# One decoder block: head-norm scaling placed one head later, gate weight sums in other slots, sum groups of 5, 5, 3 and 5

## The chip, the cores and the metric

One core of a Trainium2 chip runs the whole block. The metric is device time in microseconds (us). A run of the kernel before is given as the median of 3 runs with the lowest and the highest. Of one execution there is a profile with a trace, whose times count from the start of its span.

## The reference, cut to what matters

Batch 1, 512 tokens and 16 meta tokens ahead of them (528 positions), model width 1024, all in float32.

```
u    = rmsnorm(h, norm1_w)
proj = u @ w_in                       # q, f, i, g of HGRN2; z, xBC, dt of Mamba-2
out_a = hgrn2(q, f, i, g)             # 8 heads of 128
        # per head: o = linear recurrence(q, f, i)
        # o = o * rsqrt(mean(o*o) + eps) * norm_w * silu(g)
out_b = mamba2(z, xBC, dt)            # 16 heads of 64
h = h + concat(out_a, out_b) @ w_out
h = h + (silu(conv3(n @ w_up)[gate]) * conv3(n @ w_up)[val]) @ w_down,  n = rmsnorm(h, norm2_w)
y = rmsnorm(h, final_norm_w)[:, 16:]
```

The part at hand is the per-head norm of HGRN2 (`rsqrt(mean(o*o) + eps) * norm_w`), the gate `silu(g)`, and the weights of the gates and of the up-projection.

## The kernel before, in words

**Tiling.** Activations lie transposed, a tile is 128 channels by 528 positions. Weights come from HBM in tiles of 128 by 1024 (512 KB). A float32 product is made of three TensorE (PE) products of rounded halves: each weight tile `raw_` is split by ScalarE (ACT, line 212: `whi_`) and VectorE (DVE, line 213: `wlo_`), and each activation into `_hi` and `_lo` likewise. `ahead` (278) emits the load and split of two weight tiles ahead of their use. All weight loads go through the SyncE queue (SP).

**Order of the phases.** The first projections and Mamba-2 (to about 235 us of the span), then eight HGRN2 heads (`hgrn_head`, line 754) until about 425 us, the four gate pairs (loop at line 979), the output projection (`add_row`, 896), the up-projection (`conv3` for pairs 0 to 3, `scheme` for 4 to 21), the down-projection.

**A head.** `hgrn_head` projects f, q and i, makes decays on DVE, transposes v and k on PE (`pv`, `pk`, `pm`), copies them back on ACT (`vt`, `kt`, `mt`), forms scores on PE (`pa`, `pb`, and two columns in `pm`), masks them on DVE (line 853 writes the mask into `mt`), and multiplies (`po`, and line 866 into `pm`). ACT copies the result to `o`.

**The norm of four heads.** After heads 3 and 7 `hgrn_norm` (line 875) squares the four `o` on ACT (`osq`), sums them over channels on PE (`ph`, `phm`), takes the reciprocal root (`rh`), and then for each head stores one row to HBM (`rs_d`, line 889), loads it back spread over 128 partitions (`rb`, line 891), and multiplies `o` by it on DVE (line 892). The DMAs are SP's.

**Sums of weights.** The gates (4 pairs) and the up-projection's pairs 4 to 21 use a product scheme with seven instead of eight block products; it needs sums of weight blocks. `weight_sums` (232) makes them by accumulating DMAs from HBM to HBM (`sumsg_i`, `sums4` to `sums21`), issued by GpSimd (POOL) in groups. A group starts when a value named by its second argument is there: DVE copies a column of it into `ticks`, POOL copies that (line 237) and issues the group's DMAs, of which each stage needs the stage before. Groups of up-projection pairs before: 4 to 7 behind `ys[7]`, 8 to 11 behind `hs[3]`, 12 to 15 behind the output of head 4, 16 to 21 behind the output of head 7.

**Loading the sums.** `scheme_weights` (259) loads three tiles `w0`, `w2`, `w1` per pair, and with `w1` a fourth sum `s4` of 128 by 512 (256 KB), which is split into `s4h` (ACT, line 221) and `s4l` (DVE, line 222). All three `s4` tiles take slots of tag `ab`, of which there are 5; the heads' `vt`, `kt` and `S` use them too.

**The gates.** Per pair, PE forms blocks x, z, y, v in the order of lines 994 to 1012; ACT copies (`seed`, line 963) carry x into y and y into z; `sg` and `sgv` are the gates, multiplied into `o` on DVE (1018, 1019), and the products split into `oa`. `s4h`, `s4l` are used last, in z.

**What sets the order.** The program is written in a logical order; a scheduler with a cost model orders each engine's instructions by its own estimate of when they can start, so an edit may move nothing, or move things that it doesn't touch. Each engine then runs its list strictly in that order: an instruction that waits holds up all behind it on that engine.

Of the kernel before, what the change touches and what calls it, by code (L numbers as in the profile page):

```python
# [8 lines left out]
F32R = mybir.dt.float32r  # L9
# [45 lines left out]
DN = 1, 2, 3  # L55
D0, DK = 8, 6
NG = NH // 2
GROUPS = [("g", i) for i in range(NG)], WS[0:4], WS[4:8], WS[8:12], WS[12:], [("dn", 1)], [("dn", 2)], [("dn", 3)]
HT = 258
USUMS = {4: (0, 1), 5: (2,), 6: (3,)}  # L60
ROWS = {1: range(0, 4), 2: range(4, 8)}
NUNSC = 5

# [4 lines left out]
def tile_block(ctx: ExitStack, tc: tile.TileContext, xT, w_in, w_dt, w_out, w_up, w_down,  # L68
# [12 lines left out]
    def slot(name, n=NT, dtype=F32, parts=P, tag="m"):  # L81
        return gp.tile([parts, n], dtype, tag=tag, name=name, bufs=TAGS[tag])
# [29 lines left out]
    def col(c):  # L112
        return pt[:, c:c + 1]
# [146 lines left out]
    def scheme_weights(key):  # L260

        kind, j = key
        raw = raw_tile(key)
        hi, lo = split_tiles(key)
        if kind == "w0":
            nc.sync.dma_start(raw[:], pair_of(j)[0])
        elif kind == "w2":
            nc.sync.dma_start(raw[:], sumd[j][:, 0:2 * HK])
        else:
            n = "_".join(map(str, j)) if isinstance(j, tuple) else j  # L270
            s4 = slot(f"s4_{n}", 512, tag="ab")
            nc.sync.dma_start(s4[:], sumd[j][:, 3 * HK:])
            nc.sync.dma_start(raw[:, 0:HK], sumd[j][:, 2 * HK:3 * HK])
            nc.sync.dma_start(raw[:, HK:], pair_of(j)[1][:, HK:])
        split_weights(raw, hi, lo, slice(0, 2 * HK), V)
        if kind != "w1":
            return hi, lo
        h4, l4 = slot(f"s4h_{n}", 512, F32R, tag="ab"), slot(f"s4l_{n}", 512, F32R, tag="ab")
        last_s4[:] = [split_half(s4[:], h4[:], l4[:])]
        return hi, lo, h4, l4  # L280

# [471 lines left out]
    os_ = []  # L753
# [118 lines left out]

    rs_d = dp.tile([NH, NT], F32, name="rs_d")

    def hgrn_norm(h0):

        p0, p1 = bank(f"ph{h0}"), bank(f"phm{h0}")
        for e in range(4):
            o = os_[h0 + e]
            sq = slot(f"osq{h0 + e}", tag="L")  # L880
            A.activation(sq[:, T0:], o[:, T0:], AF.Square)
            PE.matmul(p0[32 * e:32 * e + 32, :], ones[:, 0:32], sq[:, META:], start=True, stop=True)
            PE.matmul(p1[32 * e:32 * e + 32, 0:2], ones[:, 0:32], sq[:, T0:META], start=True, stop=True)
        r = slot(f"rh{h0}", tag="L")
        log_exp(r, ((slice(T0, META), p1[:, 0:2]), (slice(META, NT), p0[:])), T0, 1.0 / P)
        for e in range(4):
            h = h0 + e
            o = os_[h]
            nc.sync.dma_start(rs_d[h:h + 1, T0:], r[32 * e:32 * e + 1, T0:])
            rb = slot(f"rb{h}", tag="L")  # L890
            nc.sync.dma_start(rb[:, T0:], rs_d[h:h + 1, T0:].partition_broadcast(P))
            V.scalar_tensor_tensor(o[:, T0:], o[:, T0:], col(C_HN + h), rb[:, T0:], ALU.mult, ALU.mult)

    tails = (slice(T0, T0 + HT), slice(NT - HT, NT))
# [42 lines left out]
    for h in range(NH):  # L937
        hgrn_head(h)
        for j in ROWS.get(h, ()):
            add_row(j, 1, obh, obl)  # L940
            if j == 3:
                weight_sums(GROUPS[2], hs[j])
        if h % 4 == 3:
            hgrn_norm(h - 3)
        for k in USUMS.get(h, ()):
            normed_sums(k)
        if h == 4:
            weight_sums(GROUPS[3], os_[h])
    weight_sums(GROUPS[4], os_[7])

    def mul(ps, hi, lo, xs, start=False):

# [23 lines left out]
    for i in range(NG):  # L976
# [38 lines left out]
        for h, g in ((2 * i, sg), (2 * i + 1, sv)):  # L1015
# [6 lines left out]
            dump(f"oa{h}", o[:])  # L1022
            oah.append(hi)
            oal.append(lo)

    u2h, u2l = [], []
    acc = None
# [383 lines left out]
```

## Time and profile before

| | |
|---|---|
| median of 3 runs | 885.41 us (882.82 to 886.45) |
| the profiled execution | 885.82 us, span 884.0 us |
| PE busy | 844.8 us (96%) |
| DVE, ACT, POOL busy | 642.1, 500.1, 140.0 us |
| mean granted TensorE clock | 0.986 |
| bytes moved by DMA | 168.73 MB, of them 62.53 MB by POOL's queue (q0) and 101.52 MB by SP's and the like (q1) |

A row of the timeline reads: start, duration, engine, line, operation, written tile <- read tiles, shapes, count, and in brackets the idle time of that engine before it and what ended that. A row of the waits reads: what waited, `<-` what for, us in total, times, longest. Buffer numbers are left out there, so `o` is any head's output and `s_g` any gate's `s4`. Rows that give "SPq" or "POOL ... DMA" show the issue of a DMA, not its transfer.

### The profile page before, as it was taken

To read this page: it belongs to the slowest core of one execution; us is meant where nothing else is said; L and a number is where in the kernel's file an instruction comes from. 1 tells how busy PE (TensorE), PEld (TensorE's weight loads), DVE (VectorE), ACT (ScalarE), POOL (GpSimd) and SP (SyncE) were. 2 spreads that over 40 slices of the span, in tenths; PEclk is the share of its full clock that TensorE was granted. 3 is DMA by queue.
4 is the path that set the end of the run, shared out by engine and by line. 5 is a ranking of instruction groups with operands and counts; after the bars stand their busy time and mean duration, and the time that the engine had idled before them with its cause. 6 is when DMAs were issued, how large, how long until landed. Compare 5 with 4: busy or idle time off the path is not lost. (4 is left out here: it accounts for less than half of the span.)

```text
span 884.0 us, 17041 instructions
## 1 busy us (share of the span) xinstructions
PE 844.8 (96%) x6864; PEld 813.1 (92%) x6864; DVE 642.1 (73%) x1106; ACT 500.1 (57%) x805; POOL 140.0 (16%) x182
## 2 busy tenths in 40 slices
PE   6999999999999994999789999999999999999996
PEld 6998898999999994999689999989999999889985
DVE  6985968788463663987366569978988888985535
ACT  8628975966232362454365555556766666764433
POOL 1300221223223212323112222200000000200000
PEclk9999999999999997899999999999999999999999
DMA  7584798886989988888669898955555555845543
GB/s 250 166 200 148 207 282 238 175 161 199 219 192 199 267 150 180 266 156 166 153 175 373 216 207 158 202 160 191 180 171 188 186 187 165 214 119 149 157 137 125
DMA packets 65839, 168.73 MB, mean 191 GB/s; under 512 B 6856, under 2 KB 11336, under 8 KB 65760
## 3 DMA queue, kind: packets, MB, share of 16 engines
q0 software_dynamic: 24800, 62.53, 36.2%
q1 hardware_dynamic: 38432, 101.52, 35.3%
q10 hardware_dynamic: 2528, 3.60, 1.2%
q8 instruction: 54, 0.88, 0.4%
q14 instruction: 25, 0.20, 0.1%
HBM read 165.47 MB, written 64.67 MB: 260 GB/s over the span
## 5 line engine op out<-in xcount | busy, mean ns | idle before, releaser
L339 PE MATMUL pj<-u_hi,whi_in 128*128 128x272 f32 (+1 forms) x624 | 132.7, 291 | 0.0
L339 PE MATMUL pj<-u_lo,whi_in 128*128 128x272 f32 (+1 forms) x624 | 131.1, 289 | 0.0
L339 PE MATMUL pj<-u_hi,wlo_in 128*128 128x272 f32 (+1 forms) x624 | 129.3, 287 | 0.0
L339 PEld LDWEIGHTS pj<-u_hi,whi_in 128*128 128x128 f32 x624 | 97.4, 190 | 2.9 <-issue 2.7
L339 PEld LDWEIGHTS pj<-u_lo,whi_in 128*128 128x128 f32 x624 | 97.4, 190 | 2.1 <-issue 1.8
L339 PEld LDWEIGHTS pj<-u_hi,wlo_in 128*128 128x128 f32 x624 | 97.2, 190 | 1.4 <-issue 1.3
L212 ACT ACTIVATE whi_in<-raw_in 128x1024 fp32r<-128x1024 f32 (+1 forms) x50 | 47.5, 951 | 73.7 <-PE pj L339 46.5
L213 DVE TENSOR_TENSOR wlo_in<-raw_in,whi_in 128x1024 fp32r<-128x1024 f32 (+1 forms) x50 | 54.5, 1090 | 26.3 <-ACT whi_in L212 22.0
L212 ACT ACTIVATE whi_w<-raw_w 128x1024 fp32r<-128x1024 f32 x54 | 57.1, 1057 | 28.2 <-PE pup L957 13.7
L213 DVE TENSOR_TENSOR wlo_w<-raw_w,whi_w 128x1024 fp32r<-128x1024 f32 x54 | 65.9, 1220 | 6.7 <-ACT whi_w L212 6.1
L237 POOL COPY tick<-ticks 128x1 f32<-128x1 f32 x8 | 11.5, 1441 | 292.8 <-DVE ticks L236 292.8
L213 DVE TENSOR_TENSOR wlo_d<-raw_d,whi_d 128x768 fp32r<-128x768 f32 x21 | 20.1, 958 | 29.6 <-ACT whi_d L212 29.6
L958 PE MATMUL pup<-n_hi,wlo_w 128*128 128x258 f32 x144 | 40.8, 283 | 0.5 <-DVE wlo_w L213 0.5
L956 PE MATMUL psn<-t1h,whi_w 128*128 128x258 f32 x144 | 41.0, 285 | 0.0
L957 PE MATMUL psn<-t1l,whi_w 128*128 128x258 f32 x144 | 40.8, 283 | 0.0
L956 PE MATMUL pup<-n_hi,whi_w 128*128 128x258 f32 x144 | 40.7, 283 | 0.0
L958 PE MATMUL psn<-t1h,wlo_w 128*128 128x258 f32 x144 | 40.7, 283 | 0.0
L957 PE MATMUL pup<-n_lo,whi_w 128*128 128x258 f32 x144 | 40.7, 283 | 0.0
L253 POOL DMA_DIRECT2D sums<-in_w_up_dram x18 | 21.4, 1187 | 111.1 <-issue 111.1
L905 DVE TENSOR_TENSOR xr<-xr,pout 128x514 f32<-128x514 f32 x16 | 11.0, 689 | 34.2 <-PE pout L339 34.2
L212 ACT ACTIVATE whi_d<-raw_d 128x768 fp32r<-128x768 f32 x21 | 17.8, 847 | 31.8 <-PE pup L1238 14.2
L212 ACT ACTIVATE whi_out<-raw_out 128x1024 fp32r<-128x1024 f32 x16 | 16.9, 1056 | 23.9 <-PE pj L339 14.5
(578 smaller groups left out, 2832.6 us busy)
## 6 DMA issues: line engine op xcount, KB each, us to landing
sums<-in_w_up_dram POOLq DMA_DIRECT2D x54, 512.0 KB, 8.7
raw_in<-in_w_in_dram SPq DMA_DIRECT2D x42, 512.0 KB, 5.9
sums<-in_w_up_dram POOLq DMA_DIRECT2D x36, 256.0 KB, 8.2
raw_w<-in_w_up_dram SPq DMA_DIRECT2D x18, 512.0 KB, 3.6
raw_w<-sums SPq DMA_DIRECT2D x18, 512.0 KB, 3.9
raw_out<-in_w_out_dram SPq DMA_DIRECT2D x16, 512.0 KB, 7.7
sumsdn<-in_w_down_dram POOLq DMA_DIRECT2D x9, 768.0 KB, 8.0
sumsg<-in_w_in_dram POOLq DMA_DIRECT2D x12, 512.0 KB, 8.7
```

The lines of the kernel that those rows point to most:

```text
L212: A.activation(hi[:, d], raw[:, d], AF.Copy)
L213: eng.tensor_tensor(lo[:, d], raw[:, d], hi[:, d].bitcast(F32), ALU.subtract)
L237: gate = G.tensor_copy(tick[:], ticks[:, n:n + 1])
L253: G.dma_start(ds[j][:, 0:2], of[j][3], accum_op=ALU.add)
L339: PE.matmul(ps[:, O + a0:O + a1], w, x[:, a0:a1], start=s, stop=e)
L905: V.tensor_tensor(hs[j][:, T0:], hs[j][:, T0:], ps[:, O + T0:O + NT], ALU.add)
L956: PE.matmul(ps, wh, xh, start=first, stop=False, skip_group_check=True)
L957: PE.matmul(ps, wh, xl, start=False, stop=False, skip_group_check=True)
L958: last_product[:] = [PE.matmul(ps, wl, xh, start=False, stop=k == KD // 2 - 1, skip_group_check=True)]
```

## The change

- `hgrn_norm` still stores and loads the factors, but the multiplications go to a new function `hgrn_scale`. For heads 0 to 3 it is called after head 4 is emitted, for heads 4 to 7 after the first gate pair.
- `USUMS`: of the sums of normed tokens (`normed_sums`), number 1 is emitted after head 5 instead of head 4.
- The `s4`, `s4h`, `s4l` of the four gates take slots of tag `m` (16 slots) instead of `ab`; those of the up-projection stay in `ab`.
- `GROUPS`: pairs 4 to 8, 9 to 13, 14 to 16 and 17 to 21. The last group waits for `os_[6]` after the gates, not for the output of head 7.

```
-GROUPS = [("g", i) for i in range(NG)], WS[0:4], WS[4:8], WS[8:12], WS[12:], [("dn", 1)], [("dn", 2)], [("dn", 3)]
+GROUPS = [("g", i) for i in range(NG)], WS[0:5], WS[5:10], WS[10:13], WS[13:], [("dn", 1)], [("dn", 2)], [("dn", 3)]
-USUMS = {4: (0, 1), 5: (2,), 6: (3,)}
+USUMS = {4: (0,), 5: (1, 2), 6: (3,)}
...
-            s4 = slot(f"s4_{n}", 512, tag="ab")
+            tag = "m" if isinstance(j, tuple) else "ab"
+            s4 = slot(f"s4_{n}", 512, tag=tag)
...
-        h4, l4 = slot(f"s4h_{n}", 512, F32R, tag="ab"), slot(f"s4l_{n}", 512, F32R, tag="ab")
+        h4, l4 = slot(f"s4h_{n}", 512, F32R, tag=tag), slot(f"s4l_{n}", 512, F32R, tag=tag)
...
             nc.sync.dma_start(rs_d[h:h + 1, T0:], r[32 * e:32 * e + 1, T0:])
-            rb = slot(f"rb{h}", tag="L")
+            rb = rbs[h] = slot(f"rb{h}", tag="L")
             nc.sync.dma_start(rb[:, T0:], rs_d[h:h + 1, T0:].partition_broadcast(P))
+
+    def hgrn_scale(h0):
+        for h in range(h0, h0 + 4):
+            o, rb = os_[h], rbs[h]
             V.scalar_tensor_tensor(o[:, T0:], o[:, T0:], col(C_HN + h), rb[:, T0:], ALU.mult, ALU.mult)
...
+        if h == 4:
+            hgrn_scale(0)
         if h % 4 == 3:
             hgrn_norm(h - 3)
...
-    weight_sums(GROUPS[4], os_[7])
...
+        if i == 0:
+            hgrn_scale(4)
+    weight_sums(GROUPS[4], os_[6])
```

What the scheduler makes of it is read from the order of each engine's instructions. The numbers behind names are buffer numbers.

**First place: DVE in head 4.** Before, from the scaling of head 1 (`o1` by `rb1`) to the mask copy into `mt0`:

```order
L892 SCALAR_TENSOR_TENSOR o1_2828<-o1_2828,pt_75,rb1_3884 128x514
L892 SCALAR_TENSOR_TENSOR o2_3356<-o2_3356,pt_75,rb2_3888 128x514
L933 TENSOR_TENSOR un0_4161<-u0_hi_311,u0_lo_312 128x514
L933 TENSOR_TENSOR un4_4163<-u4_hi_335,u4_lo_336 128x514
L912 TENSOR_TENSOR t13_u0_4165<-un0_4161 128x258
L914 TENSOR_TENSOR t13_u0_4165<-un4_4163,un0_4161 128x258
L892 SCALAR_TENSOR_TENSOR o3_3854<-o3_3854,pt_75,rb3_3892 128x514
L913 SCALAR_TENSOR_TENSOR t24_u0_4166<-un4_4163,t13_u0_4165 128x258
L933 TENSOR_TENSOR un1_4179<-u1_hi_317,u1_lo_318 128x514
L222 TENSOR_TENSOR t0l_u0_4172<-t13_u0_4165,t0h_u0_4171 128x516
L915 SCALAR_TENSOR_TENSOR t24_u0_4166<-t24_u0_4166,un4_4163 128x258
L853 COPY_PREDICATED mt0_2244<-maskA_77,pm4_4103 16x2
```

The same place in the changed program:

```order
L898 SCALAR_TENSOR_TENSOR o1_2835<-o1_2835,pt_75,rb1_3897 128x514
L898 SCALAR_TENSOR_TENSOR o2_3370<-o2_3370,pt_75,rb2_3900 128x514
L939 TENSOR_TENSOR un0_4175<-u0_hi_311,u0_lo_312 128x514
L939 TENSOR_TENSOR un4_4177<-u4_hi_335,u4_lo_336 128x514
L918 TENSOR_TENSOR t13_u0_4179<-un0_4175 128x258
L920 TENSOR_TENSOR t13_u0_4179<-un4_4177,un0_4175 128x258
L898 SCALAR_TENSOR_TENSOR o3_3868<-o3_3868,pt_75,rb3_3903 128x514
L919 SCALAR_TENSOR_TENSOR t24_u0_4180<-un4_4177,t13_u0_4179 128x258
L939 TENSOR_TENSOR un1_4482<-u1_hi_317,u1_lo_318 128x514
L222 TENSOR_TENSOR t0l_u0_4186<-t13_u0_4179,t0h_u0_4185 128x516
L921 SCALAR_TENSOR_TENSOR t24_u0_4180<-t24_u0_4180,un4_4177 128x258
L854 COPY_PREDICATED mt0_2244<-maskA_77,pm4_4113 16x2
```

Nothing moved: the four multiplications stand ahead of head 4's mask copy as before. On PE, DVE, ACT and SP all rows are the same up to the middle of head 7; only POOL's differ earlier, since its groups are others.

**Second place: ACT in head 7 and the first gate.** Before, from the copy of v to the copy of `o7`:

```order
L770 ACTIVATE v7_4965<-pj23_4916 128x528
L829 ACTIVATE vt7_5013<-pv7_5001 128x512
L828 ACTIVATE mt1_2245<-pm7_5003 16x256
L830 ACTIVATE kt7_5014<-pk7_5002 128x384
L963 ACTIVATE pyvg0_5144<-pgt0_5143 128x258
L838 ACTIVATE S7_5019<-pS7_5018 128x128
L868 ACTIVATE o7_5058<-pm7_5003 128x2
L221 ACTIVATE s4h_g_0_5157<-s4_g_0_5151 128x512
L212 ACTIVATE whi_w0_(g1_5189<-raw_w0_(g1)_5188 128x1024
L963 ACTIVATE pgt0_5143<-pyvg0_5144 128x258
L221 ACTIVATE s4h_g_1_5293<-s4_g_1_5287 128x512
L869 ACTIVATE o7_5058<-po7_5048 128x512
```

In the changed program, from the copy of v to the second `s4h`:

```order
L771 ACTIVATE v7_4972<-pj23_4923 128x528
L221 ACTIVATE s4h_g_0_5116<-s4_g_0_5110 128x512
L830 ACTIVATE vt7_5020<-pv7_5008 128x512
L829 ACTIVATE mt1_2245<-pm7_5010 16x256
L831 ACTIVATE kt7_5021<-pk7_5009 128x384
L970 ACTIVATE pyvg0_5103<-pgt0_5102 128x258
L839 ACTIVATE S7_5026<-pS7_5025 128x128
L869 ACTIVATE o7_5065<-pm7_5010 128x2
L221 ACTIVATE s4h_4_6816<-s4_4_6810 128x512
L212 ACTIVATE whi_w0_(g1_5148<-raw_w0_(g1)_5147 128x1024
L970 ACTIVATE pgt0_5102<-pyvg0_5103 128x258
L221 ACTIVATE s4h_5_6945<-s4_5_6939 128x512
```

The split of the first gate's `s4` now stands ahead of `vt7`, `mt1` and `kt7`; where the splits of the first and second gate stood, those of up-projection pairs 4 and 5 stand (`s4h_4`, `s4h_5`), again ahead of the copy of `o7`. On SP the load of `s4_g_0` goes ahead of the halves of `raw_w1_(g1)`, and the loads of `s4_4` and `s4_5` stand where those of `s4_g_0` and `s4_g_1` stood; `s4_5` takes the slot of `s4_4` and waits for its split, as `s4_g_1` did for that of `s4_g_0`. Further on, the splits of the second and third gate's `s4` stand later than before: `s4h_g_1` behind the copy `pgt1<-pyg`, `s4h_g_2` ahead of the copy `pgt2<-pyg`.

**Third place: DVE in the second and third gate.** Before, from the split of the third gate's `w0` to the scaling of head 7:

```order
L213 TENSOR_TENSOR wlo_w0_(g2_5326<-raw_w0_(g2)_5324,whi_w0_(g2_5325 128x1024
L892 SCALAR_TENSOR_TENSOR o4_4158<-o4_4158,pt_75,rb4_5084 128x514
L892 SCALAR_TENSOR_TENSOR o5_4490<-o5_4490,pt_75,rb5_5088 128x514
L1009 TENSOR_TENSOR sgv1_5282<-sg71_5283,pgt1_5278 128x258
L892 SCALAR_TENSOR_TENSOR o6_4774<-o6_4774,pt_75,rb6_5092 128x514
L213 TENSOR_TENSOR wlo_w2_(g2_5345<-raw_w2_(g2)_5343,whi_w2_(g2_5344 128x1024
L1010 TENSOR_TENSOR sgv1_5282<-sg71_5283,pyg_5279 128x258
L213 TENSOR_TENSOR wlo_w1_(g2_5421<-raw_w1_(g2)_5419,whi_w1_(g2_5420 128x1024
L892 SCALAR_TENSOR_TENSOR o7_5058<-o7_5058,pt_75,rb7_5096 128x514
```

In the changed program, from the scaling of head 4 to the split of `w1`:

```order
L898 SCALAR_TENSOR_TENSOR o4_4168<-o4_4168,pt_75,rb4_5091 128x514
L213 TENSOR_TENSOR wlo_w0_(g2_5289<-raw_w0_(g2)_5287,whi_w0_(g2_5288 128x1024
L898 SCALAR_TENSOR_TENSOR o5_4479<-o5_4479,pt_75,rb5_5094 128x514
L222 TENSOR_TENSOR s4l_g_1_5257<-s4_g_1_5250,s4h_g_1_5256 128x512
L1016 TENSOR_TENSOR sgv1_5245<-sg71_5246,pgt1_5241 128x258
L898 SCALAR_TENSOR_TENSOR o6_4781<-o6_4781,pt_75,rb6_5097 128x514
L898 SCALAR_TENSOR_TENSOR o7_5065<-o7_5065,pt_75,rb7_5100 128x514
L213 TENSOR_TENSOR wlo_w2_(g2_5308<-raw_w2_(g2)_5306,whi_w2_(g2_5307 128x1024
L1017 TENSOR_TENSOR sgv1_5245<-sg71_5246,pyg_5242 128x258
L213 TENSOR_TENSOR wlo_w1_(g2_5384<-raw_w1_(g2)_5382,whi_w1_(g2_5383 128x1024
```

The scaling of head 7, which needs the load of `rb7`, moved ahead of the splits of `w2` and `w1` of the third gate. On PE the ten matmuls that need `wlo_w1_(g2` moved ahead of the 24 others of that gate (x and y) behind which they stood. In the output projection, ACT's and DVE's splits of `raw_out` 4 to 7 stand one tile earlier, and the split of `raw_up_0` stands two tiles earlier.

More of the change, by code (lines that the diff above doesn't have):

```diff
@@ L873, in tile_block @@
     rs_d = dp.tile([NH, NT], F32, name="rs_d")
+    rbs = {}
     def hgrn_norm(h0):
@@ L887, in hgrn_norm @@
             h = h0 + e
-            o = os_[h]
             nc.sync.dma_start(rs_d[h:h + 1, T0:], r[32 * e:32 * e + 1, T0:])
-            rb = slot(f"rb{h}", tag="L")
+            rb = rbs[h] = slot(f"rb{h}", tag="L")
             nc.sync.dma_start(rb[:, T0:], rs_d[h:h + 1, T0:].partition_broadcast(P))
+    def hgrn_scale(h0):
+        for h in range(h0, h0 + 4):
+            o, rb = os_[h], rbs[h]
             V.scalar_tensor_tensor(o[:, T0:], o[:, T0:], col(C_HN + h), rb[:, T0:], ALU.mult, ALU.mult)
```

## The prediction, as it went on record

> **What bounds the kernel now.** I read the page first, for who is busy.
>
> ```profile
> span 884.0 us, 17041 instructions
> PE 844.8 (96%) x6864; PEld 813.1 (92%) x6864; DVE 642.1 (73%) x1106; ACT 500.1 (57%) x805; POOL 140.0 (16%) x182
> ```
>
> PE is busy for 844.8 of 884.0 us, and the change gives it the same matmuls. So it can only win or lose PE's idle time, 39 us, and what follows from that. The profiled execution took 885.82 us, 1.82 more than its span and 0.41 above the median of 885.41; I sum against 885.82 and take the 0.41 off at the end. The second view is PE's waits:
>
> ```profile
> PE pm L866 <- DVE mt L853: 11.2, 1, 11.2
> PE ph L882 <- ACT osq L881: 4.9, 1, 4.9
> PE pgt L956 <- ACT pyg L963: 2.1, 2, 1.8
> PE pyvg L956 <- ACT pgt L963: 1.6, 1, 1.6
> PE pout L339 <- DVE wlo_out L213: 1.4, 1, 1.4
> ```
>
> These five, 21.2 us, lie where the change works: the first in head 4, three in the gates, the last in the output projection. The third view follows the first wait, in the timelines of DVE and SP:
>
> ```profile
> 341.54 0.75 DVE L892 SCALAR_TENSOR_TENSOR o<-o,pt,rb 128x514 f32<-128x514 f32 x1 [8.85 <-DMA rb<-rs_d]
> ...
> 350.22 0.75 DVE L892 SCALAR_TENSOR_TENSOR o<-o,pt,rb 128x514 f32<-128x514 f32 x1 [1.96 <-DMA rb<-rs_d]
> ...
> 352.77 0.14 DVE L853 COPY_PREDICATED mt<-maskA,pm 16x2 f32<-16x2 int32 x1
> ```
>
> ```profile
> 330.44 0.93 SPq L889 DMA_DIRECT2D rs_d<-rh  x3
> 335.07 2.02 SPq L891 DMA_DIRECT2D rb<-rs_d  x3
> ...
> 344.98 0.32 SPq L891 DMA_DIRECT2D rb<-rs_d  x1
> ```
>
> The stored rows are 4.6 us under way (330.44 to 335.07), the first spread row 6.5 (335.07 to 341.54), the last is issued at 344.98 and used at 350.22. DVE stands in its list until then, and the 0.14 us mask copy behind it, at 352.77, is what PE needs. This is a chain of DMA latencies, held by DVE's order. The fourth view is the gates, ACT and SP:
>
> ```profile
> 415.05 0.59 ACT L770 ACTIVATE v<-pj 128x528 f32<-128x528 f32 x1
> 416.44 0.60 ACT L829 ACTIVATE vt<-pv 128x512 f32<-128x512 f32 x1 [0.80 <-PE pv L822]
> ...
> 426.12 0.63 ACT L221 ACTIVATE s4h_g<-s_g 128x512 fp32r<-128x512 f32 x1 [5.26 <-DMA s_g<-sumsg]
> ...
> 434.42 0.63 ACT L221 ACTIVATE s4h_g<-s_g 128x512 fp32r<-128x512 f32 x1 [6.45 <-DMA s_g<-sumsg]
> ```
>
> ```profile
> 411.02 0.33 SPq L268 DMA_DIRECT2D raw_w_(g1)_5207<-sumsg  x1
> ...
> 417.58 10.24 SPq L272 DMA_DIRECT2D s_g<-sumsg  x2
> ```
>
> ```profile
> DMA to landing us min/median/max: 3.2/5.1/8.5
> ```
>
> The last row is the view of the tiles `s_g`. The first `s4` is issued at 417.58 and lands before 426.12 (the 8.5), the second is issued once its slot is free (417.58 + 10.24 = 427.8) and lands at 434.4. ACT waits for each, and what stands behind, the copies `pgt` and `o7`, is what PE waits for.
>
> **The change part by part.**
>
> *Scaling of heads 0 to 3: 0.* The call stands one head later, but the order shows DVE's twelve instructions around it unmoved, and SP's loads too. So the 11.2 us wait is the same chain; only the traffic beside it can differ. That traffic is POOL's sums; the ticks give their pace:
>
> ```profile
> 207.66 2.86 POOL L237 COPY tick<-ticks 128x1 f32<-128x1 f32 x1 [14.22 <-DVE ticks L236]
> 277.21 1.16 POOL L237 COPY tick<-ticks 128x1 f32<-128x1 f32 x1
> 357.56 0.26 POOL L237 COPY tick<-ticks 128x1 f32<-128x1 f32 x1 [6.38 <-DVE ticks L236]
> ...
> 426.89 0.81 POOL L258 DMA_DIRECT2D sums<-sums  x1 [3.15 <-issue]
> 460.44 0.53 POOL L237 COPY tick<-ticks 128x1 f32<-128x1 f32 x1 [32.74 <-DVE ticks L236]
> ```
>
> Four pairs take 277.21 - 207.66 = 69.6 us, 17.4 a pair; the third group's four 426.89 + 0.81 - 357.56 = 70.1, 17.5 a pair. With 5, 5, 3 the second group ends near 207.7 + 10 x 17.5 = 383 and the third near 383 + 53 = 436, instead of 428. At 330 to 352 the queue is busy in both cases, in an earlier stage of the same kind. I take 0, between -3 and +4: four latencies in series, each about 1 us off. [...]
>
> *First gate's `s4` in its own slot: +0.5 net.* It is now issued behind `raw_w_(g1)` at 411.02, so near 411.4, and with the 8.5 us of its kind lands at 419.9. But its split now stands behind `v` (done 415.64) and ahead of `vt`. ACT then does `vt` at 420.5 instead of 416.44, 4.1 us late, and `mt` behind it, for which PE waits. With the least landing, 3.2 us, nothing is late. The later waits take this back:
>
> ```profile
> 417.34 0.49 PE L834 MATMUL pS<-mt 128*128 128x128 f32 x2 [0.38 <-ACT mt L828]
> ...
> 428.03 0.39 PE L956 MATMUL pyvg<-t0h_u,whi_w_(g 128*128 128x258 f32 x1 [1.57 <-ACT pgt L963]
> ...
> 436.25 1.63 PE L882 MATMUL ph<-osq,cf 128*32 128x512 f32 x2 [4.95 <-ACT osq L881]
> ```
>
> In the places of the two old splits stand those of pairs 4 and 5, with loads from the same place of SP's list and the same slot between them. So `o7` is again released at about 434.4, PE's `ph` at 436.25, and 4.1 late on PE is less than 1.57 + 4.95 = 6.5 of waits ahead of it. Net 0 where the landings repeat, -5 if `s4_4` and `s4_5` land in 3.2, +3 if POOL's longer third group slows both by 1.5; I take +0.5.
>
> *Third gate's `s4h` leaves its old place: -0.6.*
>
> ```profile
> 444.66 0.28 PE L958 MATMUL pvg<-t0h_u,wlo_w_(g 128*128 128x258 f32 x1
> 446.72 0.52 PE L956 MATMUL pgt<-u_hi,whi_w_(g 128*128 128x258 f32 x1 [1.79 <-ACT pyg L963]
> 447.04 0.42 PE L957 MATMUL pgt<-u_lo,whi_w_(g 128*128 128x258 f32 x1
> ```
>
> A 0.6 us split (the rows above) leaves the queue ahead of the copy `pyg`, so the 1.79 shrinks to 1.2.
>
> *Scaling of heads 4 to 7 in one row: +2.1.*
>
> ```profile
> 452.25 0.35 SPq L891 DMA_DIRECT2D rb<-rs_d  x1
> ```
>
> ```profile
> 454.95 0.75 DVE L892 SCALAR_TENSOR_TENSOR o<-o,pt,rb 128x514 f32<-128x514 f32 x1 [0.92 <-DMA rb<-rs_d]
> 455.62 1.22 DVE L213 TENSOR_TENSOR wlo_w_(g<-raw_w_(g2)_5343,whi_w_(g 128x1024 fp32r<-128x1024 f32 x1
> 456.75 0.42 DVE L1010 TENSOR_TENSOR sgv<-sg,pyg 128x258 f32<-128x258 f32 x1
> ```
>
> ```profile
> 457.49 0.28 PE L956 MATMUL pvg<-t0h_u,whi_w_(g 128*128 128x258 f32 x1
> ```
>
> Head 7's factor was issued at 452.25 and used behind everything that PE needs. Now it stands ahead of both splits, and ahead of `raw_w0_(g3)` on SP, so about 1 us earlier, at 451.3. I give it 4.3 us, between the least landing above, 3.2, and the 5.2 from SP's 344.98 to DVE's 350.22: there at 455.6. Then its scaling 0.75, `wlo_w2` 1.22, the addition `sgv` 0.42, `wlo_w1` 1.22: 459.2. PE comes to the third of these matmuls at about 457.7, less the 0.6 above, so 457.1, and waits 2.1. Bounds: 0 if the factor lands by 453.5, +4 if it lands at 457.5.
>
> *Second and third gate's later `s4h`: +1.* The third gate's is loaded behind its neighbour's `w1`, issued about 1 us later than before, and ACT now has it ahead of the copy that PE needs:
>
> ```profile
> 458.33 0.32 SPq L273 DMA_DIRECT2D raw_w_(g3)_5552<-sumsg  x1
> ```
>
> ```profile
> 462.60 0.28 PE L956 MATMUL pgt<-t0h_u,whi_w_(g 128*128 128x258 f32 x1
> ```
>
> Issued near 460, landed in 3.2 to 5.1, split in 0.6: ready between 464 and 466. PE, which was there at 462.60 and is 1.5 late by now, arrives at 464. So 0 to +2, and I take 1.
>
> *Output projection: -1.4.* The wait on `wlo_out` came because ACT split `raw_out` 6 behind `up0h`, which stood behind the squares of the fifth output tile; both now stand ahead of that tile's squares, so the split can run some us sooner and the wait goes (0 if its load is late instead):
>
> ```profile
> 507.41 1.14 ACT L221 ACTIVATE up0h<-raw_up 128x512 fp32r<-128x512 f32 x2
> 508.45 1.05 ACT L212 ACTIVATE whi_out<-raw_out 128x1024 fp32r<-128x1024 f32 x1
> ```
>
> *At nothing:* the last group starts near 481 instead of 460.44 but has five pairs, so it ends near 481 + 88 = 569 instead of 460 + 105 = 565, and its pairs 17 to 21 are the last used; the normed sums 1 don't move on DVE; `s4` 4 to 6 are merely loaded earlier.
>
> *Clock: +0.7.* Behind the 1.79 us wait the matmuls follow at 0.2 instead of 0.12 us for about 16 of them (447.04 against 444.66: 0.42 to 0.28 in duration), near 1.5 us lost; two new waits of 1 to 2.3 us may each catch it, or not, as behind the 1.57. So 0 to 3. [...]
>
> Sum: 885.82 + 0 + 0.5 - 0.6 + 2.1 + 1 - 1.4 + 0.7 = 888.1, less 0.41: 887.7.
>
> **The rivals.**
>
> *Slower: POOL's longer groups slow SP's chains.* Groups of five put the second and third group beside the loads of `rb0` to `rb3` (330 to 350) and of `s4_4`, `s4_5` (417 to 434). If each of the four serial landings in head 4 takes 1 us more and each of the two `s4` 1.5, the first wait is 15 and `ph` comes 3 later: 887.7 + 4 + 3 - 0.5 = 894. It decides against me from +2.1 on, half a microsecond on each landing. For it: 426.89 moves to 436, so the queue is no longer empty when `s4_5` loads. Against: 17.4 and 17.5 us a pair in two groups say that the load is even.
>
> *Faster: the gates' DMAs meet an empty queue.* If the third group, now of three pairs, ends before 417, `s4_4` and `s4_5` land in 3.2 us each instead of 8.5 and 6.6; PE's `ph` wait goes and 1.57 with it: 887.7 - 6.5 = 881 or below. It needs 14 us a pair in the second group. For it: only three pairs. Against: the ticks above.
>
> *Faster: the change does what it says.* If head 4's mask copy no longer stood behind the factors, the 11.2 would go: 887.7 - 11.2 = 876.5, and somewhat less for the clock. Against it stands the unmoved order of DVE.
>
> **How the numbers follow.** A measurement of this kernel can tell about 0.5% from no change, 881.0 to 889.8 around 885.41. My forecast, no change, +2.3, gets 0.47 for its inner part (its own range, by the bounds above, is 882 to 892); its upper end beyond 889.8 gets 0.08. The slower rival gets 0.28, the gates' one 0.11, the one of the words 0.06. So faster 0.17, same 0.47, slower 0.36. Leaving the outermost out, 879 to 895.
>
> **What would show it.** Right: DVE's waits for `rb` in head 4 still near 13 us and PE's behind the mask copy near 11; a new wait of PE at `pS` near 417 and a shorter one at `ph`; a new one at `pvg` near 457; none at `wlo_out`. Wrong: the 11.2 us wait gone or halved, or past 14; `ph` released before 432 or after 439; the third group's last DMA before 420.

## The result, and the profile after

The changed kernel takes 888.24 us (median of 12 runs, 886.88 to 893.39), the kernel before 883.9 us on the same chip (12 runs, 879.38 to 887.39): ratio 1.0057, 95% interval 1.0034 to 1.008. Forecast were 887.7 us, 2.3 above the 885.41 that the prediction set out from; the two medians here differ by 4.3. The profiled execution took 888.65 us with a span of 886.9; against the 884.0 of before that is 2.9 more. The page's first lines and PE's waits, all that touch the change:

```profile
span 886.9 us, 17039 instructions
PE 849.8 (96%) x6864; PEld 817.4 (92%) x6864; DVE 643.0 (73%) x1106; ACT 500.6 (56%) x805; POOL 138.6 (16%) x182
```

```profile
PE pm L867 <- DVE mt L854: 5.6, 1, 5.6
PE pS L835 <- ACT mt L829: 4.2, 1, 4.2
PE pgt L965 <- DVE wlo_w_(g L213: 3.4, 1, 3.4
PE pgt L963 <- DVE sgv L1016: 1.7, 1, 1.7
PE pgt L963 <- ACT pyg L970: 1.6, 1, 1.6
PE pvg L965 <- DVE wlo_w_(g L213: 1.4, 1, 1.4
...
PE pout L340 <- ACT sg L1021: 0.7, 1, 0.7
PE pgt L963 <- ACT pgt L970: 0.6, 1, 0.6
```

The wait in head 4 is 5.6 instead of 11.2; those at `ph` and `wlo_out` are gone; new are 4.2 at `pS` and three in the second and third gate. These rows sum to 19.2 us. The same stretch before had the five quoted in the prediction, 21.2, one of 0.4 at `pS` and one of 0.2 at `pgt`. So the waits fell by 2.6 us and the time rose by 2.9: PE's busy time, with the same 6864 matmuls, is 5.0 us longer. Most of that is the clock: the mean granted clock was 0.986 before and 0.981 after, so 884.0 x 0.014 = 12.4 and 886.9 x 0.019 = 16.9 us were lost to it, 4.5 more. Apart from the program's first and last microseconds, the windows view gives a clock of 0.50 from 344.42 to 358.08, 436.58 to 440.00 and 446.82 to 450.24 before, 20.5 us together, and from 344.17 to 354.41, 415.85 to 426.09 and 453.40 to 463.64 after, 30.7 us. One row of each kernel's windows shows where (the last three columns are granted clock, DMA share, GB/s). Before:

```profile
410.00:464.00 54.00, 44.81 (x347) 41.47 (x346) 29.46 (x50) 28.09 (x45) 9.29 (x13) 0.94 0.70 164
```

After:

```profile
410.00:464.00 54.00, 41.62 (x281) 37.98 (x281) 24.77 (x42) 24.80 (x41) 9.01 (x10) 0.81 0.87 189
```

From head 7 to the third gate PE lost 54 x 0.06 = 3 us of clock before and 54 x 0.19 = 10 after, and the record has 281 instead of 347 matmuls in that time, beside a DMA share of 0.87 instead of 0.70. In head 4 it was the other way round: from 341 to 360 us the clock was 0.64 before and 0.73 after, 6.8 and 5.1 us lost.

**Head 4.** DVE's list is the one of before, but the loads land sooner. SP and DVE after:

```profile
330.84 0.87 SPq L891 DMA_DIRECT2D rs_d<-rh  x3
332.05 1.29 SPq L893 DMA_DIRECT2D rb<-rs_d  x3
...
340.19 0.32 SPq L893 DMA_DIRECT2D rb<-rs_d  x1
```

```profile
335.38 0.75 DVE L898 SCALAR_TENSOR_TENSOR o<-o,pt,rb 128x514 f32<-128x514 f32 x1 [2.29 <-DMA rb<-rs_d]
...
345.01 0.75 DVE L898 SCALAR_TENSOR_TENSOR o<-o,pt,rb 128x514 f32<-128x514 f32 x1 [1.35 <-DMA rb<-rs_d]
347.56 0.14 DVE L854 COPY_PREDICATED mt<-maskA,pm 16x2 f32<-16x2 int32 x1
```

The stored rows take 1.2 us instead of 4.6, the first spread row 3.3 instead of 6.5; the mask copy comes at 347.56 instead of 352.77.

**Head 7.** SP issues the first gate's `s4` at 406.90, and ACT has its split ahead of `vt`:

```profile
410.51 0.59 ACT L771 ACTIVATE v<-pj 128x528 f32<-128x528 f32 x1
415.21 0.63 ACT L221 ACTIVATE s4h_g<-s_g 128x512 fp32r<-128x512 f32 x1 [4.11 <-DMA s_g<-sumsg]
415.75 0.58 ACT L830 ACTIVATE vt<-pv 128x512 f32<-128x512 f32 x1
416.23 0.36 ACT L829 ACTIVATE mt<-pm 16x256 f32<-16x256 f32 x1
```

The load is 8.3 us under way, ACT stands idle 4.11, and PE 4.2 at `pS`. Head 4's five microseconds are mostly spent here: PE passes `pS` at 416.63, before at 417.34.

**Gates.** DVE in the third gate:

```profile
450.04 0.75 DVE L898 SCALAR_TENSOR_TENSOR o<-o,pt,rb 128x514 f32<-128x514 f32 x1 [5.41 <-DMA rb<-rs_d]
450.71 1.22 DVE L213 TENSOR_TENSOR wlo_w_(g<-raw_w_(g2)_5287,whi_w_(g 128x1024 fp32r<-128x1024 f32 x1
...
456.54 0.75 DVE L898 SCALAR_TENSOR_TENSOR o<-o,pt,rb 128x514 f32<-128x514 f32 x1 [0.86 <-DMA rb<-rs_d]
457.21 1.22 DVE L213 TENSOR_TENSOR wlo_w_(g<-raw_w_(g2)_5306,whi_w_(g 128x1024 fp32r<-128x1024 f32 x1
458.34 0.42 DVE L1017 TENSOR_TENSOR sgv<-sg,pyg 128x258 f32<-128x258 f32 x1
458.68 1.22 DVE L213 TENSOR_TENSOR wlo_w_(g<-raw_w_(g2)_5382,whi_w_(g 128x1024 fp32r<-128x1024 f32 x1
```

The first row is head 4's output, scaled ahead of the split of `w0`: DVE waits 5.41 for `rb4`, and PE 3.4 for `wlo_w0`. Before, the two stood the other way round. The last rows are the queue that the prediction counted out for head 7. PE's last squares sum of the heads (`ph`) starts at 433.06, 3.2 us ahead of before, and the kernel ends 2.9 behind: the price is paid from there on, in the second to fourth gate.

### The profile page after: what moved, and what is told of

It reads as the page before. It is cut to its first block, busy times and chain, and to the rows that moved or that the text cites. A ratio compares the mean times of both kernels' runs of the same rounds, so it can differ in the third digit from the quotient of the medians.

```text
span 886.9 us, 17039 instructions
## 1 busy us (share of the span) xinstructions
PE 849.8 (96%) x6864; PEld 817.4 (92%) x6864; DVE 643.0 (73%) x1106; ACT 500.6 (56%) x805; POOL 138.6 (16%) x182
## 5 line engine op out<-in xcount | busy, mean ns | idle before, releaser
L237 POOL COPY tick<-ticks 128x1 f32<-128x1 f32 x8 | 10.8, 1346 | 293.3 <-DVE ticks L236 293.3
L253 POOL DMA_DIRECT2D sums<-in_w_up_dram x18 | 21.2, 1178 | 113.8 <-issue 113.8
L212 ACT ACTIVATE whi_out<-raw_out 128x1024 fp32r<-128x1024 f32 x16 | 16.9, 1058 | 25.4 <-PE pj L340 14.4
```

The lines of the kernel that those rows point to most:

```text
L212: A.activation(hi[:, d], raw[:, d], AF.Copy)
L237: gate = G.tensor_copy(tick[:], ticks[:, n:n + 1])
L253: G.dma_start(ds[j][:, 0:2], of[j][3], accum_op=ALU.add)
```

## The experiments

All ratios are against the kernel before on the same chip. A profile is of one execution: those of the groups alone, of the slots with the last group, and of the forced scaling with a short third group lie 3.2, 3.9 and 4.9 us below the median of their kernel, and that of the last experiment 3.5 above, so their single waits needn't be the usual ones. The order of the instructions tells something first: with the scaling and `USUMS` taken out of the changed kernel, so that only groups and slots are left, all five engines have the same rows as with them. The part that gives the change its first words moves nothing here. The theory to begin with was that groups and slots have one effect each, of opposite sign; the rival that both act through what POOL's DMAs run beside.

**Groups alone.**

```
+GROUPS = [("g", i) for i in range(NG)], WS[0:5], WS[5:10], WS[10:13], WS[13:], [("dn", 1)], [("dn", 2)], [("dn", 3)]
...
-    weight_sums(GROUPS[4], os_[7])
...
             oal.append(lo)
+    weight_sums(GROUPS[4], os_[6])
```

> The kernel before with nothing but the new groups of sums: 5, 5, 3 and 5 pairs, the last one behind the output of head 6 after the gates. Theory O (order and groups have one effect each): the groups alone shorten PE's wait behind head 4's mask copy from 11.2 us to about 5.6, because other DMAs of the sums run beside the loads of rb0 to rb3, and leave the gates as they were: about 5 us faster, ratio 0.994. Theory Q (queue): the groups do that, but the third group's end, which moves from 428 to about 443 us, also slows the loads of s4 and of rb4 to rb7 in the gates: PE's waits between 437 and 462 us add 4 us or more to those of the kernel before, and the ratio is 0.998 to 1.002. Theory N (noise): the wait in head 4 differs from execution to execution whatever the groups; then it is near 11 here and the ratio is 1.000 to 1.002.

Measured 0.9988 (0.9966 to 1.0009). Head 4 waited 6.1, and the gates did not stay as they were:

```profile
348.35 0.58 PE L866 MATMUL pm<-mt 128*128 128x2 f32 x2 [6.05 <-DVE mt L853]
...
427.19 1.05 PE L882 MATMUL ph<-osq,cf 128*32 128x512 f32 x2 [1.66 <-ACT osq L881]
436.68 0.58 PE L955 MATMUL pgt<-u_hi,whi_w_(g 128*128 128x258 f32 x1 [2.36 <-ACT pyg L962]
...
450.09 0.56 PE L955 MATMUL pgt<-u_hi,s4h_g 128*128 128x258 f32 x1 [4.04 <-DVE sgv L1008]
```

Theory Q, then: the shorter wait is there, and the ratio lies in its band, not at 0.994.

**Slots alone.**

```
+            tag = "m" if isinstance(j, tuple) else "ab"
+            s4 = slot(f"s4_{n}", 512, tag=tag)
...
+        h4, l4 = slot(f"s4h_{n}", 512, F32R, tag=tag), slot(f"s4l_{n}", 512, F32R, tag=tag)
```

> The kernel before with nothing but the gates' s4, s4h and s4l in slots of tag m. Theory O: head 4 waits 11.2 us as before, PE waits about 4 us at pS near 420 because the split s4h_g_0 stands ahead of vt7, mt1 and kt7 on ACT, and the second and third gate wait 5 to 7 us for rb6, rb7 and s4_g_1, which are issued later and are needed earlier in the lists: about 6 us slower, ratio 1.006 to 1.008. Theory Q: the wait at pS comes, but it is paid back by the waits behind it, and the second gate's loads meet an empty queue once the third group has ended at 428 us: no wait of over 1.5 us between 440 and 462 us, ratio 1.000 to 1.003.

Measured 1.0134 (1.0106 to 1.0162), worse than either theory and than the whole change. `pS` waited 2.9. The largest wait in the gates is at the fourth one. POOL and ACT there:

```profile
456.02 0.75 POOL L250 DMA_DIRECT2D sums<-in_w_up_dram  x1
...
464.59 0.71 POOL L250 DMA_DIRECT2D sums<-in_w_up_dram  x1 [6.07 <-issue]
...
473.05 0.71 POOL L250 DMA_DIRECT2D sums<-in_w_up_dram  x1 [4.27 <-issue]
```

```profile
484.16 0.63 ACT L221 ACTIVATE s4h_g<-s_g 128x512 fp32r<-128x512 f32 x1 [5.71 <-DMA s_g<-sumsg]
```

The last group of sums starts at 455.39 (before, at 460.44), but the fourth `s4`, issued at 473.37, is now loaded beside it and takes 10.8 us; PE waits 5.4 at 484.84. In the changed kernel that group starts at 487.25, and the wait is not there.

**Scaling alone.**

```
+        if h == 4:
+            hgrn_scale(0)
...
+        if i == 0:
+            hgrn_scale(4)
```

> The kernel before with nothing but the scaling of heads 0 to 3 called after head 4 and that of heads 4 to 7 after the first gate pair. The last group of sums then waits for the output of head 7 unscaled, so it may start near 435 us instead of 460. Both theories: the order of DVE around head 4 is unmoved, so PE waits about 11 us there. Theory O: the scaling of heads 4 to 7 now stands behind the splits of the third gate's weights on DVE, so the 1.8 us wait and the slow clock behind it may go; the ratio is 0.998 to 1.001. Theory Q: the last group, 25 us earlier, puts its DMAs beside rb4 to rb7 and the gates' s4 and makes those land 2 us later each: ratio 1.002 to 1.006.

Measured 1.0104 (1.0067 to 1.0141), above both bands. Head 4 waited 11.6 us, as both theories said. The last group waits for `o7` unscaled and starts at 425.51, and its twelve first DMAs run beside the gates' loads. PE waits for the splits of the gates' weights, where before it had none over half a microsecond from 447 to 500 us:

```profile
466.87 0.39 PE L965 MATMUL pgt<-u_hi,whi_w_(g 128*128 128x258 f32 x1 [1.63 <-ACT whi_w_(g L212]
468.13 0.58 PE L967 MATMUL pgt<-u_hi,wlo_w_(g 128*128 128x258 f32 x1 [0.76 <-DVE wlo_w_(g L213]
```

The sign is theory Q's, but its reason isn't in the trace: from 440 to 485 us neither ACT nor DVE waits for a DMA. The split that ends the first of these waits, `whi_w` of the fourth gate at 465.77, stands in ACT's list behind the third gate's `sgv` and `sg` (465.28); before, it stood behind the second gate's (458.56). So PE waits here for another order of the lists. Whether the earlier group adds to the price isn't shown.

**Scaling forced behind the mask.**

`masked` holds DVE's last copy of the scores of a head; `issue_after` queues what follows behind it on its engine.

```
+        masked[:] = [V.tensor_copy(s3[64:96, :, 96:128], b3[96:128, :, 32:64])]
...
         if h == 4:
+            with tc.issue_after(masked[0].ins):
+                hgrn_scale(0)
```

> The kernel before, with the scaling of heads 0 to 3 queued on DVE behind the last mask copy of head 4, so that the words of the change come true there; groups and slots as before. Both theories: no wait of PE behind head 4's mask copy mt, since nothing ahead of that copy needs rb0 to rb3. If the 11.2 us are the whole price, the run is 11 to 12 us faster (with the slow clock behind the wait), ratio 0.986 to 0.988. The rival: something else is late next, a DVE instruction of head 4 or the copies on ACT, and holds PE for 4 to 8 us in the same stage: ratio 0.991 to 0.996.

Measured 0.9929 (0.99 to 0.9959), 6.3 us, the rival's band. Head 4's wait is gone; a wait of 2.3 at `pk` (361.96) is the next thing late, the rival's mechanism at half its price. PE passes `pS` of head 7 at 407.44, 9.9 us earlier than before, and the span, 876.0, is 8.0 shorter: from 410 to 437 us the clock is 0.87 instead of 0.99, behind waits of 3.42 at `pyvg` and 3.44 at `ph`.

**Slots, and the last group behind the gates.** To the edit of the slots comes

```
-    weight_sums(GROUPS[4], os_[7])
...
             oal.append(lo)
+    weight_sums(GROUPS[4], os_[6])
```

> The kernel before with the gates' s4 in slots of tag m and the last group of sums behind the output of head 6 after the gates; the groups keep 4, 4, 4 and 6 pairs, so head 4 waits 9 to 11 us. Theory L (last group): with the slots alone the ratio was 1.0134, since the last group's first DMAs, issued from 456 us, ran beside the load of the fourth gate's s4, for which PE waited 5.4 us at 484.84 and then ran on at the slow clock. Here they start behind the gates, that wait goes, and the ratio is 1.003 to 1.008, near that of the whole change (1.0057). Theory S (sizes): what the whole change is better by than the slots alone is the shorter wait in head 4 from the groups' sizes; then the ratio stays at 1.011 to 1.014 here.

Measured 1.0044 (1.0019 to 1.007): theory L. The wait at the fourth gate is gone, and of the slots' 1.3% some 0.6 are left (1.0044 over the 0.9982 that the last group's move gives by itself, below). On PE, DVE, ACT and SP this kernel has the changed kernel's order through all the gates, but POOL's third group ended at 420.94, not at 443.15, and DVE's row for head 4 reads

```profile
444.12 0.76 DVE L893 SCALAR_TENSOR_TENSOR o<-o,pt,rb 128x514 f32<-128x514 f32 x1 [0.18 <-DMA rb<-rs_d]
```

`rb4`, issued at 439.90, was there after 4.2 us; in the changed kernel, issued at 441.09, after 9.0. `s4_g_1` took 4.2 here (441.14 to 445.36) and 10.2 there (443.14 to 453.32). In these two executions the same loads at the same place of the list took twice as long beside the end of the third group.

**Sizes alone, last group alone.** The first is

```
-GROUPS = [("g", i) for i in range(NG)], WS[0:4], WS[4:8], WS[8:12], WS[12:], [("dn", 1)], [("dn", 2)], [("dn", 3)]
+GROUPS = [("g", i) for i in range(NG)], WS[0:5], WS[5:10], WS[10:13], WS[13:], [("dn", 1)], [("dn", 2)], [("dn", 3)]
```

and the second the last block's two lines, without the slots.

> The kernel before with groups of 5, 5, 3 and 5 pairs, the last one at its old place behind the scaled output of head 7. Theory S: the wait in head 4 is 5 to 7 us instead of 11.2, nothing else changes: ratio 0.993 to 0.996. Theory L: the same wait in head 4, but it gains little in the end, since the third group ends near 443 us beside the loads of rb4 to rb7 and of s4, and the last one starts there: ratio 0.998 to 1.003. If the wait in head 4 is 9 us or more, the short waits of the two runs with these sizes so far (6.1 and 5.6 us) were chance.

> The kernel before with the last group of sums behind the output of head 6 after the gates, sizes and slots as before. Both theories: head 4 waits 9 to 12 us. Theory L: the gates' loads in the kernel before come ahead of 460 us, where its last group starts, so there is little to win: ratio 0.998 to 1.002. Theory S: no change at all, 0.999 to 1.001. Both would be wrong if the last group, now some 25 us later with six pairs, were late for the up-projection: PE would wait for sums between 580 and 860 us, ratio over 1.004.

Measured 1.0008 (0.9985 to 1.0031) and 0.9982 (0.9959 to 1.0005): theory L for the sizes, whose interval leaves out theory S's 0.993 to 0.996. The last group alone doesn't tell the two apart, since its interval takes in most of both bands. Head 4 waited 7.3 with the new sizes and 12.9 with the old (expected were 5 to 7 and 9 to 12). With the new sizes PE passes `pS` of head 7 at 413.70, 3.6 us earlier than before, and waits again at `ph` (3.02), `pyg` (1.79 and 3.32) and `whi_out` (1.28); its mean clock over 12 runs is 0.9854, before 0.987. The gain of head 4 is spent on the loads behind it.

**Forced scaling with the new groups.** The edit of the forced scaling on top of that of the groups.

> The groups of the changed kernel (5, 5, 3, 5, the last one after the gates) with the scaling of heads 0 to 3 queued behind the last mask copy of head 4, and the gates' s4 in their old slots. The forced scaling alone gave 0.9929, the groups alone 0.9988. Theory S: both act on the same wait of head 4, so together they give no more than the forced scaling: 0.991 to 0.995. Theory L: the wait of head 4 goes by the scaling, and the groups free the second half of the gates from the last group's DMAs: 0.988 to 0.992. If the third group's end near 443 us costs the gates more than that, it is 0.994 or above.

Measured 0.9955 (0.9932 to 0.9979): the case named last, though the interval reaches into theory S's band. PE's waits, and ACT's ahead of them:

```profile
403.72 0.49 PE L837 MATMUL pS<-mt 128*128 128x128 f32 x2 [0.38 <-ACT mt L831]
418.46 0.58 PE L968 MATMUL pyvg<-t0h_u,whi_w_(g 128*128 128x258 f32 x1 [5.63 <-ACT pgt L975]
426.97 1.92 PE L887 MATMUL ph<-osq,cf 128*32 128x512 f32 x2 [3.28 <-ACT osq L886]
```

```profile
416.56 0.63 ACT L221 ACTIVATE s4h_g<-s_g 128x512 fp32r<-128x512 f32 x1 [9.33 <-DMA s_g<-sumsg]
...
425.14 0.63 ACT L221 ACTIVATE s4h_g<-s_g 128x512 fp32r<-128x512 f32 x1 [6.72 <-DMA s_g<-sumsg]
```

PE passes `pS` 9.5 us ahead of the kernel with the groups alone (413.21), and `ph` at the same time (427.19 there). ACT stands for the first gate's `s4`, issued at 404.66 and split at 416.56, and then for the second's; `pgt` and `osq` are behind them. What ends PE's waits here is not its own pace but those loads, beside the third group.

**The changed kernel with a shorter tail.** In the changed kernel:

```
-GROUPS = [("g", i) for i in range(NG)], WS[0:5], WS[5:10], WS[10:13], WS[13:], [("dn", 1)], [("dn", 2)], [("dn", 3)]
+GROUPS = [("g", i) for i in range(NG)], WS[0:5], WS[5:9], WS[9:12], WS[12:], [("dn", 1)], [("dn", 2)], [("dn", 3)]
```

> The changed kernel with groups of 5, 4, 3 and 6 pairs instead of 5, 5, 3 and 5: the second group keeps its place beside the loads of rb0 to rb3 in head 4, the third ends near 415 to 425 us instead of 443, and the last one starts behind the gates as before. Theory T (tail): the groups' sizes gain 4.7 us in head 4 and lose as much in the gates, because the third group's last DMAs, to 443 us, run beside the loads of s4, rb4 to rb7 and the gates' weights. Then the wait of head 4 stays at 5.5 to 7.5 us, PE's waits between 437 and 500 us fall from 7.5 us to about 4, and the ratio is 0.997 to 1.002. Theory P (place): the gates lose because the loads stand at other places of the lists and are asked for later, whatever POOL does; then the waits there remain at 6 us or more and the ratio is 1.004 to 1.008.

Measured 1.0047 (1.002 to 1.0075), in theory P's band. Head 4 waited 7.5. The third group ended at 425.92; the waits from 437 to 500 us fell from 9.5 to 5.1 (1.84, 2.53, 0.69), as theory T said in kind. But `pS` still waited 4.13 and `ph` 2.04, and the last group of six pairs, which ends at 592.31, held a weight of the up-projection (PE waits 1.96 at 586.56). What the tail alone is worth stays open within the interval.

**Forced scaling, short third group.** Old slots, the forced scaling, the last group behind the gates, and

```
-GROUPS = [("g", i) for i in range(NG)], WS[0:4], WS[4:8], WS[8:12], WS[12:], [("dn", 1)], [("dn", 2)], [("dn", 3)]
+GROUPS = [("g", i) for i in range(NG)], WS[0:4], WS[4:8], WS[8:11], WS[11:], [("dn", 1)], [("dn", 2)], [("dn", 3)]
```

> The kernel before with the scaling of heads 0 to 3 queued behind the last mask copy of head 4, groups of 4, 4, 3 and 7 pairs, and the last group behind the gates; old slots. Theory T: head 4 has no wait, the third group ends near 405 us, so the first gate's s4 and the loads behind it land in 3 to 5 us, and what the forced scaling wins is not waited for again at pyvg and ph (9 us in the run with forced scaling and the new groups, 7 us in that with forced scaling alone): ratio 0.983 to 0.989. Theory P: the waits at pyvg and ph, 7 to 9 us together, remain, since the list of SP issues those loads no earlier: ratio 0.991 to 0.995.

Measured 0.9887 (0.9844 to 0.993), 873.01 us, the fastest kernel here. The ratio is at the upper end of theory T's band and its interval reaches into theory P's; the waits decide for theory T. The third group ended at 408.32. The first `s4` took 8.0 us (404.12 to 412.10) and not 3 to 5, the second, behind it, about 3, and the two waits are

```profile
414.00 0.39 PE L969 MATMUL pyvg<-t0h_u,whi_w_(g 128*128 128x258 f32 x1 [1.13 <-ACT pgt L976]
418.33 1.04 PE L887 MATMUL ph<-osq,cf 128*32 128x512 f32 x2 [1.07 <-ACT osq L886]
```

`pS` is at 403.75 as in the run above, `ph` 8.6 us earlier. The mean clock of its six runs is 0.9937, before 0.987.

**POOL silent in head 4 and in the gates.** In the kernel before:

```
+GROUPS = [("g", i) for i in range(NG)], WS[0:4], WS[4:7], WS[7:11], WS[11:], [("dn", 1)], [("dn", 2)], [("dn", 3)]
...
-                weight_sums(GROUPS[2], hs[j])
...
-            weight_sums(GROUPS[3], os_[h])
-    weight_sums(GROUPS[4], os_[7])
+            weight_sums(GROUPS[2], os_[h])
...
             oal.append(lo)
+    weight_sums(GROUPS[3], os_[6])
+    weight_sums(GROUPS[4], os_[6])
```

> The kernel before with POOL silent from the end of the first group, near 277 us, until the output of head 4 is there: groups of 4, 3, 4 and 7 pairs, the second behind head 4, the third and the last behind the gates. Theory T: the chain of rs_d and rb loads in head 4 meets no DMA of the sums, each landing takes 2 to 4 us, and PE's wait there is 2 to 5 us instead of 11; the gates meet none either: PE's waits from 410 to 462 us, 9 us before, are 5 or less, and the ratio is 0.985 to 0.992, unless the late sums hold the up-projection (waits for sums behind 600 us). Theory P: the chain's latencies are those of SP's list and of the weights' loads, so head 4 waits 9 us or more without the sums too, ratio 0.997 to 1.001.

Measured 1.0147 (1.01 to 1.0193), and it tells most about head 4:

```profile
343.88 0.38 PE L866 MATMUL pm<-mt 128*128 128x2 f32 x2 [1.32 <-DVE mt L853]
406.21 0.49 PE L834 MATMUL pS<-mt 128*128 128x128 f32 x2 [0.38 <-ACT mt L828]
427.86 0.39 PE L955 MATMUL pgt<-u_hi,whi_w_(g 128*128 128x258 f32 x1 [2.25 <-ACT pyg L962]
...
503.50 0.41 PE L339 MATMUL pup<-u2h,up0h 128*128 128x258 f32 x2
...
644.92 0.58 PE L955 MATMUL pup<-t0h,whi_w 128*128 128x258 f32 x1 [16.02 <-ACT pup L962]
```

Without the sums' DMAs the same chain on the same list lets PE wait 1.32 us, below theory T's 2 to 5, and of the gates' waits 2.25 is the only one over half a microsecond. The first matmul of the up-projection starts at 503.50, before at 524.16: PE is 20.7 us ahead by then. The late sums take all of it back and more: 16.02 at one place of the up-projection alone, where ACT stands 18.65 us for an `s4` whose sum isn't ready. So the ratio, outside theory T's band, is the case that theory T excepted. What this run doesn't give is a way to have the sums early and the loads undisturbed.

**Only the first gate's `s4` in a new slot.**

```
-            tag = "m" if isinstance(j, tuple) else "ab"
+            tag = "m" if j == ("g", 0) else "ab"
```

> The changed kernel with only the first gate's s4, s4h and s4l in slots of tag m, those of the other gates back in ab. Its order is that of the kernel with the groups alone (0.9988) on PE, and on ACT too but for the split s4h_g_0, which stands ahead of vt7, mt1 and kt7. Theory B (first gate pays): the wait at pS, about 4 us, and the slow clock behind it are the price of the slots; they remain, and the ratio is 1.003 to 1.006, that of the whole change (1.0057). Theory D (second and third gate pay): the wait at pS is paid back by shorter waits at pyvg and ph, as predicted (+0.5 us), and the price lies in the later loads and splits of the second and third gate; those are back at their places here, and the ratio is 0.998 to 1.001.

Measured 1.0004 (0.9977 to 1.0031): theory D's band. It is weaker than hoped, since `pS` waited 1.38 and not 4: head 4 waited 9.28 in this profile, so PE came to `pS` 2.7 us later than in the changed kernel, and the `s4` landed at the same time (its split at 415.11, there at 415.21). That the other gates' slots make the difference to 1.0057 rests on two intervals that only just part.

**Taken together.** Of the whole change (1.0057), the scaling and `USUMS` move nothing, the new sizes alone give 1.0008, the groups alone 0.9988, and the slots with the last group, at the old sizes, already 1.0044. So the price is that of the slots, most likely those of the second to fourth gate (1.0004 without them), which change the order of loads, splits and scaling there. How much of it is the order itself and how much the slower loads beside the third group isn't parted: with a third group that ends 17 us earlier the waits there fell by 4.4 us, and the ratio was still 1.0047.

## Why the prediction was right, and where it was not

The number and the sign held, and the number in part by luck. First, the forecast set out from 885.41, the median of 3 runs; over 12 runs on the same chip the kernel before takes 883.9. Forecast was a loss of 2.3 us, measured one of 4.3, and the lower start hides most of the difference. Second, two large errors of opposite sign stand inside the sum: the terms on waits add up to +1.6, and PE's waits fell by 2.6; the clock was put at +0.7, and the profiles show 4.5.

- **Scaling of heads 0 to 3 (0, bounds -3 to +4): wrong in size.** The order was unmoved and the chain the same, as written, but the wait halved (11.2 to 5.6), which the prediction itself named as a sign that it would be wrong. The step that failed is "the queue is busy in both cases, in an earlier stage of the same kind". Four more profiles with a first group of five show 6.1, 7.3, 7.5 and 9.3 us beside the changed kernel's 5.6; five with the old ones 9.5, 10.0, 11.2, 11.6 and 12.9; the silent one 1.3. So the sums' DMAs make most of this wait, and the new sizes shorten it by about 4 us in the mean (7.1 against 11.0). What they change is the stage that runs beside the loads: with the old sizes POOL's lines 256 and 258 in all five profiles (before, eight issues from 333.86 to 350.34), with the new ones lines 253 and 254 in all five (after, two of each from 331.98 to 344.61). The bytes moved from 330 to 350 us hardly differ, 193 and 184 GB/s. That it is the stage is argued from this coincidence, and it isn't all: the changed kernel and the one with only the first gate's slot are one program up to head 7, and waited 5.6 and 9.3, with line 253 issued at 331.98 in the one and at 338.24 in the other.
- **First gate's `s4` (+0.5 net): the wait right, and for the reason given.** Predicted was a wait of 4.1 at `pS` near 417: 4.2 at 416.63, behind a load of 8.3 us. It was paid back (the 1.57 and 4.95 behind it are gone), but otherwise than predicted: the splits of `s4_4` and `s4_5` (422.54 and 428.76) no longer wait for their loads, and `ph` starts at 433.06 unwaited, not at 436.25. The kernel with this slot alone gave 1.0004, if with a shorter wait.
- **Third gate's `s4h` (-0.6):** the wait of 1.79 became 1.57, a gain of 0.2.
- **Heads 4 to 7 in one row (+2.1): right where it was counted, short by a row.** The third `pvg` waited 1.4, head 7's scaling came at 456.54 (predicted 455.6). But in the order shown with the change, `o4` had moved ahead of `wlo_w0` as well; that was not priced and cost 3.4, since `rb4` took 9.0 us beside the third group.
- **Later `s4h` (+1):** waits of 1.7 and 0.6. **Output projection (-1.4):** the wait is gone, with 0.7 at `sg` in its place.
- **Clock (+0.7): the term that carries the result.** It counted less than one slow stretch of 3.4 us more (3.42 in the profile of before), at 1.5 us each; around the wait of 4.2 at `pS` and around those of 3.4, 1.7 and 1.4 in the gates the clock was at half for 10.2 us each time. Over 12 runs the mean clock was 0.9827, over 35 runs of the kernel before, on another chip, 0.987: 15.4 against 11.5 us lost, 3.9 more, where the change costs 4 to 5 (a lost clock counts only where PE has work, so this is an upper bound).
- **POOL's pace: the reading left a group out.** 17.4 and 17.5 us a pair are the first and third group. The second, between the ticks shown, took 277.21 to 351.18, 18.5 a pair, so the load was not even. In the changed kernel the second group's last issue ended at 389.6 and the third's at 444.0, not at 383 and 436.
- **Rivals.** That POOL's longer groups slow SP's chains was right in the gates and had the wrong sign in head 4. The gates' empty queue never came: the third group's last issue is at 443.15, not ahead of 417. That the change does what it says was rightly refused; forced, it gains 0.7%, about 6 us and not 11.2, since `pk` and the clock in the gates come next.

## What to carry to other kernels

A wait on a chain of small DMAs is not a constant of the chain: 1.3, 7 or 11 us (the last two in the mean of five) were the same four loads beside no transfers of a background queue, beside one of its stages and beside another, so ask of every such wait what runs beside it, and of every regrouping of background work which loads it will now meet. Compare whole rows of the order with those of before, not only the ones the change names; the swap that cost 3.4 us stood in the row next to the one that was priced. And a gain ahead of a stage that waits for loads is worth only what those loads allow: 9.5 us of lead were gone at the next such wait until the background group ended earlier. Moving background work out of the way only helps if its results are still in time: 20.7 us of lead were lost again to sums that came late.

## What the runs showed of the hardware that was not expected

Apart from their ends, in the profiles of before and after the half clock (0.50 in the windows view) came in stretches of 3.42 us (436.58 to 440.00 and 446.82 to 450.24 before), of 10.24 (all three after) and of 13.66 (344.42 to 358.08 before), one length, three times it and four times; behind two waits of 3.4 us it began only 1.4 us after PE had resumed (421.40 with forced scaling, 453.40 after). PE in the kernel with the new sizes alone, behind a wait of 1.79 us:

```profile
440.07 0.39 PE L956 MATMUL pgt<-u_hi,whi_w_(g 128*128 128x258 f32 x1 [1.79 <-ACT pyg L963]
440.30 0.28 PE L957 MATMUL pgt<-u_lo,whi_w_(g 128*128 128x258 f32 x1
440.42 0.38 PE L958 MATMUL pgt<-u_hi,wlo_w_(g 128*128 128x258 f32 x1
440.60 0.42 PE L956 MATMUL pgt<-u_hi,whi_w_(g 128*128 128x258 f32 x1
```

The second still takes 0.28, as the matmuls at a clock of 1.00 do (450.26 and on, before), then 0.42 holds until 443.61, 3.2 us; in the profile of before, behind a wait of the same length, from the start at 446.72 to 450.05, 3.3 us. With forced scaling, behind a wait of 3.42 us, it began at 421.40 after 1.4 us of matmuls of 0.28 each. In the changed kernel the stretch behind the 4.2 us wait lasted until 426.09, by the windows view 10.2 us, three such lengths. In the stretch of 3.3 us before the matmuls follow at 0.215 us instead of the 0.12 behind it, so it does 3.3 / 0.215 = 15 in place of 27 and costs 1.5 us besides the wait. Waits of 1.79 us had such a stretch behind them in these two profiles. Behind the wait of 1.57 us at 428.03 in the profile of before no such stretch came: the clock is 1.00 from 428 to 434 us.
